# Gate and up projections by seven block products for eight, in one planned order with the first down blocks

## The chip, the cores and the metric

The kernel runs on one core of a Trainium2 chip. Its engines are TensorE (PE, with its weight loads as PEld), VectorE (DVE), ScalarE (ACT), GpSimd (POOL) and SyncE (SP), which issues the DMAs. The metric is the device time of one execution in microseconds (us), lower being better; the median of several runs is given with its spread.

## What is computed

One layer of a streaming encoder, on 1024 prompt frames and 32 sample frames (T = 1056 together), with a model width of 1024, 8 attention heads, 8 retention heads and a feed-forward width of 2816. All inputs and outputs are float32.

```python
h   = rmsnorm(x, g_norm);  z = h @ w_in            # q, k, v, retention q, k, v, gates
mix = sigmoid(gate_a) * diff_attention(...) + sigmoid(gate_r) * retention(...)
x   = x + mix @ w_o
h   = rmsnorm(x, g_ffn)
x   = x + (silu(h @ w_ff_gate) * (h @ w_ff_up)) @ w_ff_down
gate = sigmoid(rmsnorm(x, g_ple) @ w_ple_gate)
x   = x + gate * (p @ w_ple)
```

The change is in the lines from `x + mix @ w_o` to the product with `w_ff_down`.

## The kernel before, in words

**Precision.** TensorE gets float16 operands. Each float32 matrix is scaled by a power of two and split into a high and a low float16 part, and a product is made of three matmuls: high by high, high by low, low by high (`mm3`, L440 to L443). The scale of a block of weights comes from its largest magnitude: a reduction on DVE, then `partition_all_reduce` on POOL (L285), then a few one-column operations on DVE (`weight_scale`, L278). In the attention stage the scales of the input weights come from sums of squares (L393) that are spread over the partitions through TensorE (`spread_max`, L257).

**Attention stage.** Input projection, attention, retention and their gates are written as generators that say what they need next (an engine and an estimated time, a buffer, an event). The class `Flow` (L80) orders them: it always takes the step that can start first, and among equals the one with the lower priority number, and the instructions go to PE, DVE, ACT and POOL in that order under `manual_schedule` (L1384). At the end come the products for the last gate (`ple`, L1277), while the output weights `wo` (L1216, L1225) are loaded.

**Output projection** (from 1104.85 us on). Activations lie transposed, 128 features on the partitions and frames along the row. Three chunks c of 352 columns, and for each eight output blocks m of 128 features: 8 x 3 matmuls of 352 columns into a PSUM bank. DVE adds x (L1451), the sum goes to DRAM (`x1_d`, L1453), ACT squares it (L358), DVE sums the squares (L360). The norm of a chunk (`norm_steps`, L319) runs while TensorE works on the next: four column sums on TensorE (L328), DVE (L331), the power -0.5 on POOL (L333), a diagonal on DVE (L335), a broadcast on TensorE (L342); then the chunk is scaled and split into `xh1` (L349, L350, L352).

**Gate and up.** 22 blocks j of 128 features, loaded in 11 pairs (`load_gu`, L1398: DMA L1404, reduction L1406, splits L1410 and L1411). For each block and each of three chunks, a gate product and an up product of 8 x 3 matmuls of 352 columns (`gu_mm`, L1421), then `gu_out` (L1471): tanh on ACT (L1474), two products on DVE (L1475, L1476), a high part on ACT (L1478) and a low part on DVE (L1479), into `aT`, which holds all 22 blocks in SBUF.

**Down** (1679.18 to 1916.50 us). Eight output blocks m, three chunks, 22 x 3 matmuls of 352 columns each (L1520 to L1522); the weights of the next block (`load_dn`, L1481) are prepared meanwhile. The last gate follows.

Outside the attention stage the order is that of the framework, in the program's sequence, with the norm steps put between products by `step()` (L314). Three SBUF tiles hold split weights (`wtile`), two hold raw ones (`stage`), seven PSUM banks take products (`psb`, L1390) and one the sums (`pss`).

Of the kernel before, what the change touches and what calls it, by code (L numbers as in the profile page):

```python
# [33 lines left out]
NCH = 3  # L34
EPS = 1e-6
# [8 lines left out]
def _f(x):  # L44
    return float(x)
# [132 lines left out]
def kernel(  # L178
# [35 lines left out]
    mix_d = dram.tile([H, P, 2, T], F16, name="mix_d")  # L214

# [41 lines left out]
    def spread_max(amax, n, tag):  # L257


        yield ("wait", "id")  # L260
        yield ("get", "o")
        yield M(0.1)
        pt = ps_o.tile([P, 512], F32, tag="o", name="mt")
# [14 lines left out]
    def weight_scale(amax, n, gi, tag, pool=True, norm=False):  # L278
# [3 lines left out]
        if pool:  # L282
            yield G(0, 0.1)
            ar = sm(n, tag + "ar", 3)
            nc.gpsimd.partition_all_reduce(ar, amax, P, ABSMAX)  # L285
            yield from p2of(p2, ar, n, tag)
        else:
            ar = yield from spread_max(amax, n, tag)
            yield from p2of(p2, ar, n, tag, norm)
            yield ("put", "o")  # L290
# [4 lines left out]
        nc.vector.tensor_scalar(out=s, in0=s, scalar1=_f(2.0 ** -50) if norm else 16384.0, scalar2=None, op0=ALU.mult)  # L295
        d = sm(n, tag + "d", 6)
        if gi is None:
            nc.vector.tensor_scalar(out=d, in0=p2, scalar1=_f(2.0 ** -14), scalar2=None, op0=ALU.mult)
# [20 lines left out]
    def norm_steps(acc, dg, tag, split, late=0):  # L319

        pending.extend([lambda: None] * late)
        B = CH // 4
        box = []

        def first():
            ps = pss.tile([P, 512], F32, tag="ss", name="ss")
            for b in range(4):
                nc.tensor.matmul(out=ps[0:B, CH + b:CH + b + 1], lhsT=acc[:, b * B:(b + 1) * B], rhs=ones32[:, 0:1],  # L328
                                 start=True, stop=True)
            v = sm(4, tag + "v")  # L330
            nc.vector.tensor_scalar(out=v[0:B], in0=ps[0:B, CH:CH + 4], scalar1=_f(1.0 / D), scalar2=EPS, op0=ALU.mult, op1=ALU.add)  # L331
# [8 lines left out]
        def second():  # L340
            ps, d = box
            nc.tensor.matmul(out=ps[:, 0:CH], lhsT=ones32[0:B], rhs=d[0:B], start=True, stop=True)  # L342
            split(ps[:, 0:CH])
# [10 lines left out]
    def square_sum(pool, xf, k0, k1, acc):  # L354

        for k in range(k0, k1):
            sq = acc if k == 0 else pool.tile([P, CH], F32, tag="sq", name="sq")
# [97 lines left out]
    with ExitStack() as pa:  # L455
# [83 lines left out]
        def const_b():  # L539
# [10 lines left out]
            yield ("delay", 2.0)  # L550

# [760 lines left out]
        def stream():  # L1312
# [85 lines left out]
    def load_gu(jp):  # L1398
        w = wtile()[:, 0:KD * 1024].rearrange("p (j u a k c) -> p j u a k c", j=2, u=2, a=2, k=KD)
        hds = []  # L1400
        for jj in range(2):
            j = 2 * jp + jj
            st = stage()[:, 0:KD * 256].rearrange("p (k u c) -> p k u c", k=KD, u=2)
            nc.sync.dma_start(out=st, in_=wgu[j])  # L1404
            am = sm(2, "gam2", 3)
            nc.vector.tensor_reduce(out=am, in_=st.rearrange("p k g c -> p g k c"), axis=AX.XY, op=ALU.max,  # L1406
                                    apply_absolute_value=True)
            s, d = weight_scale_now(am, 2, 1, "gu")
            for u in range(2):
                nc.scalar.activation(w[:, jj, u, 0], st[:, :, u], AF.Copy, scale=s[:, u:u + 1])  # L1410
                nc.vector.scalar_tensor_tensor(out=w[:, jj, u, 1], in0=st[:, :, u], scalar=s[:, u:u + 1],  # L1411
                                               in1=w[:, jj, u, 0], op0=ALU.mult, op1=ALU.subtract)

            nc.vector.tensor_scalar(out=rf[:, j:j + 1], in0=d[:, 0:1], scalar1=_f(2.0 ** 55), scalar2=d[:, 1:2],
                                    op0=ALU.mult, op1=ALU.mult)
            hd = sm(1, "hdg", 6)
            nc.vector.tensor_scalar(out=hd, in0=d[:, 0:1], scalar1=0.5, scalar2=None, op0=ALU.mult)
            hds.append(hd)
        return w, hds

    def gu_mm(wt, jj, c):  # L1421
        cs = slice(c * CH, (c + 1) * CH)
        out = []
        for u in range(2):
            ps = bank()
            for k in range(KD):
                mm3(ps, wt[:, jj, u, 0, k], wt[:, jj, u, 1, k], xh1[:, k, 0, cs], xh1[:, k, 1, cs], k == 0, k == KD - 1)
            step()
            out.append(ps)
        return out  # L1430

    with ExitStack() as pb:
        wk = pb.enter_context(DT(name="wkB", bufs=2))
        xc = pb.enter_context(DT(name="xcB", bufs=2))
        wos = tail["wos"]

        mixs = xh1 = tail["mixs"]
        for c in range(NCH):
            c0 = c * CH
            xf = xc.tile([P, KD, CH], F32, tag="xf", name="xf")  # L1440
            nc.sync.dma_start(out=xf, in_=xT[:, :, c0:c0 + CH])
            acc = wk.tile([P, CH], F32, tag="acc", name="acc")
            for m in range(KD):
                ps = bank()
                wt, d = wos[m // 4]
                ms = slice(m % 4 * P, (m % 4 + 1) * P)
                for k in range(KD):
                    mm3(ps, wt[:, k, 0, ms], wt[:, k, 1, ms], mixs[:, k, 0, c0:c0 + CH], mixs[:, k, 1, c0:c0 + CH],
                        k == 0, k == KD - 1)
                step()  # L1450
                nc.vector.scalar_tensor_tensor(out=xf[:, m], in0=ps, scalar=d[m % 4 // 2], in1=xf[:, m],  # L1451
                                               op0=ALU.mult, op1=ALU.add)
                nc.sync.dma_start(out=x1_d[m, :, c0:c0 + CH], in_=xf[:, m])  # L1453
                square_sum(wk, lambda k: xf[:, k], m, m + 1, acc)

            def split(rs, c0=c0, xf=xf):
                for k in range(KD):
                    split_x(wk.tile([P, CH], F32, tag="sx", name="sx", bufs=4), xh1[:, k, 0, c0:c0 + CH], xh1[:, k, 1, c0:c0 + CH],
                            xf[:, k], k, rs, 1)

            norm_steps(acc, lambda: wk.tile([P, CH], F32, tag="dg", name="dg"), "nb", split, 1)
        nxt = load_gu(0)
        ahead = [gu_mm(nxt[0], 0, c) for c in range(2)]


    with ExitStack() as pc:
        apool = pc.enter_context(DT(name="apool", bufs=1))
        wk = pc.enter_context(DT(name="wkC", bufs=2))
        aT = apool.tile([P, NF, 2, T], F16, name="aT")

        def gu_out(j, c, hd, pg, pu):  # L1471
            cs = slice(c * CH, (c + 1) * CH)
            th = wk.tile([P, CH], F32, tag="sq", name="th")
            nc.scalar.activation(th, pg, AF.Tanh, scale=hd)  # L1474
            nc.vector.scalar_tensor_tensor(out=th, in0=th, scalar=1.0, in1=pg, op0=ALU.add, op1=ALU.mult)  # L1475
# [213 lines left out]
```

## Time and profile before

| | |
|---|---|
| runs, median | 2012.34 us of 3 (2011.31 to 2012.55) |
| the profiled execution | 2011.19 us, its span 2009.2 us |
| granted TensorE clock, mean | 0.994 |
| PE busy | 1953.9 us, 97% |
| DVE busy | 1328.2 us, 66% |
| ACT busy | 925.7 us, 46% |
| POOL busy | 553.8 us, 28% |
| DMA | 137.52 MB, 68 GB/s in the mean |
| matmul instructions recorded | 13577 |

Busy is the time in which an engine has at least one instruction under way. Matmuls overlap, and a row's duration of one matmul is longer than the distance to the next start; so paces are read from starts. A few per cent of matmul records are missing in a trace, so counts come from the code. A row of the timeline gives start, length, engine, line, operation, result and operands, count, and in brackets the idle time of the engine before it with what ended it.

### The profile page before, as it was taken

The page shows a single profiled execution, that of the slowest core. Times are in us where ns is not written, and L with a number is a line of the kernel's source. Part 1 is how long each engine was busy: PE and PEld are TensorE (multiplying, and loading weights), DVE is VectorE, ACT ScalarE, POOL GpSimd, SP SyncE. Part 2 cuts the span into 40 slices and gives each one's busy share as a digit, 9 for nine tenths or more (in the row PEclk, how much of TensorE's full clock was granted, in tenths as well). Part 3 has the DMA queues.
Part 4 walks back from the last instruction along what each step waited for, and adds up shares of the span by engine and source line. Part 5 has one row for each costly group of instructions (what it writes and reads, how often), then busy time and mean ns, then how long its engine had stood idle before and what let it go on. Part 6 is the DMA issues. An engine that isn't in the chain of part 4 may idle for free.

```text
span 2009.2 us, 35867 instructions
## 1 busy us (share of the span) xinstructions
PE 1953.9 (97%) x13577; PEld 1204.5 (60%) x13577; DVE 1328.2 (66%) x3465; ACT 925.7 (46%) x2406; POOL 553.8 (28%) x1059
## 2 busy tenths in 40 slices
PE   5899999999999999999999999999999999999999
PEld 2465565655655555555565566666666666666665
DVE  6887878787777877877987666454445543543364
ACT  6676666666666666666665233222223221111132
POOL 4654445454453545444441011000000000000010
PEclk9999999999999999999999999999999999999999
DMA  5121202112021111211216431211111103111131
GB/s 190 69 71 51 80 25 65 54 52 67 26 74 57 47 62 32 75 59 28 81 32 243 160 118 46 81 43 42 43 43 53 49 29 116 58 58 43 43 123 51
DMA packets 67148, 137.52 MB, mean 68 GB/s; under 512 B 24832, under 2 KB 49536, under 8 KB 59040
## 3 DMA queue, kind: packets, MB, share of 16 engines
q1 hardware_dynamic: 66976, 135.25, 20.3%
q8 instruction: 106, 1.74, 0.4%
q14 instruction: 66, 0.54, 0.1%
HBM read 108.74 MB, written 26.48 MB: 67 GB/s over the span
## 4 chain that ended last, share of the span: by engine, by line
PE 81%; DVE 9%; ACT 3%; POOL 3%; DMA 2%; issue 1%; SPq 0%; POOLq 0%; ACTq 0%; DVEq 0%
PE ps L441 10%; PE ps L442 10%; PE ps L443 10%; PE pj L688 8%; PE pj L690 8%; PE pj L689 8%; PE ps L1522 4%; PE ps L1521 4%; PE ps L1520 4%; PE sc L825 2%; PE sc L828 1%; PE t L872 1%; PE pj L699 1%; PE t L1020 1%; ACT p L843 1%
## 5 line engine op out<-in xcount | busy, mean ns | idle before, releaser
L441 PE MATMUL ps<-mixs,w 128*128 128x352 f16 x1248 | 391.5, 314 | 1.5 <-DVE pws L1298 1.5
L689 PE MATMUL pj<-w,xh 128*128 128x512 f16 x1024 | 389.6, 381 | 3.1 <-DVE w L434 3.1
L688 PE MATMUL pj<-w,xh 128*128 128x512 f16 x1024 | 390.8, 382 | 1.8 <-ACT w L432 1.8
L442 PE MATMUL ps<-mixs,w 128*128 128x352 f16 x1248 | 391.3, 314 | 0.0
L443 PE MATMUL ps<-mixs,w 128*128 128x352 f16 x1248 | 391.2, 313 | 0.0
L690 PE MATMUL pj<-w,xh 128*128 128x512 f16 x1024 | 389.6, 380 | 0.0
L441 PEld LDWEIGHTS <-w 128*128 128x128 f16 x1488 | 146.3, 98 | 79.5 <-DVE pws L1298 1.9
L442 PEld LDWEIGHTS <-w 128*128 128x128 f16 x1488 | 146.1, 98 | 77.3 <-issue 1.3
L443 PEld LDWEIGHTS <-w 128*128 128x128 f16 x1488 | 146.1, 98 | 77.3
L690 PEld LDWEIGHTS <-xh 128*128 128x128 f16 x1024 | 100.5, 98 | 125.8 <-issue 6.1
L1522 PE MATMUL ps<-aT,w 128*128 128x352 f16 x528 | 165.0, 313 | 0.0
L1521 PE MATMUL ps<-aT,w 128*128 128x352 f16 x528 | 165.0, 313 | 0.0
L1520 PE MATMUL ps<-aT,w 128*128 128x352 f16 x528 | 165.0, 313 | 0.0
L843 ACT ACTIVATE p<-sc,nb,scs 128x256 f32<-128x256 f32 (+7 forms) x128 | 106.1, 829 | 99.4 <-POOL nb L837 66.4
L688 PEld LDWEIGHTS <-xh 128*128 128x128 f16 x1024 | 101.2, 99 | 72.6 <-issue 1.0
L689 PEld LDWEIGHTS <-xh 128*128 128x128 f16 x1024 | 100.6, 98 | 71.6 <-issue 2.9
L1478 ACT ACTIVATE aT<-th 128x352 f16<-128x352 f32 x66 | 32.5, 494 | 201.2 <-DVE th L1476 195.4
L835 DVE TENSOR_REDUCE nm<-sc 128x2 f32<-128x256 f32 (+6 forms) x112 | 102.8, 918 | 23.5 <-PE sc L828 23.2
L285 POOL PARTITION_ALL_REDUCE guar<-gam x22 | 8.9, 406 | 364.5 <-DVE gam L1406 351.6
L1476 DVE SCALAR_TENSOR_TENSOR th<-th,ps 128x352 f32<-128x352 f32 x66 | 34.3, 519 | 101.8 <-PE ps L443 101.7
L1475 DVE SCALAR_TENSOR_TENSOR th<-th,ps 128x352 f32<-128x352 f32 x66 | 34.2, 518 | 89.7 <-ACT th L1474 89.6
L1474 ACT ACTIVATE th<-ps,hdg 128x352 f32<-128x352 f32 x66 | 36.2, 550 | 114.1 <-PE ps L443 113.8
(400 smaller groups left out, 4209.5 us busy)
## 6 DMA issues: line engine op xcount, KB each, us to landing
st<-in_win_dram SPq DMA_DIRECT2D x30, 1024.0 KB, 4.9
st<-in_wgu_dram SPq DMA_DIRECT2D x22, 1024.0 KB, 5.1
st<-in_wdn_dram SPq DMA_DIRECT2D x16, 704.0 KB, 4.4
out_dram<-kv SPq DMA_DIRECT2D x64, 128.0 KB, 1.7
mixs<-mix_d SPq DMA_DIRECT2D x8, 528.0 KB, 6.8
pw_d<-pws SPq DMA_DIRECT2D x12, 352.0 KB, 3.6
xf<-in_xT_dram SPq DMA_DIRECT2D x3, 1408.0 KB, 7.2
x_d<-xf SPq DMA_DIRECT2D x24, 176.0 KB, 2.2
```

What stands on the lines that cost most here:

```text
L441: nc.tensor.matmul(out=ps, lhsT=wh, rhs=ah, start=first, stop=False)
L442: nc.tensor.matmul(out=ps, lhsT=wh, rhs=al, start=False, stop=False)
L443: nc.tensor.matmul(out=ps, lhsT=wl, rhs=ah, start=False, stop=last)
L688: nc.tensor.matmul(out=ps, lhsT=xhi, rhs=w[:, k, 0], start=(k == 0), stop=False)
L689: nc.tensor.matmul(out=ps, lhsT=xhi, rhs=w[:, k, 1], start=False, stop=False)
L690: nc.tensor.matmul(out=ps, lhsT=xh[:, k, 1, t0:t0 + P], rhs=w[:, k, 0], start=False, stop=(k == KD - 1))
L825: nc.tensor.matmul(out=o, lhsT=q4[:, m, 0:R], rhs=kts[:, m], start=True, stop=False)
L835: nc.vector.tensor_reduce(out=nm[0:R, mc], in_=pv, axis=AX.X, op=ALU.max, negate=True)
L843: nc.scalar.activation(pt[0:R, 0:NK], ps[0:R, p0:p0 + NK], AF.Exp, bias=nb[0:R, m:m + 1], scale=sc_ap[0:R], accum_out=Z[0:R, m:m + 1])
L1520: nc.tensor.matmul(out=ps, lhsT=wt[:, 0, j], rhs=aT[:, j, 0, cs], start=(j == 0), stop=False)
L1521: nc.tensor.matmul(out=ps, lhsT=wt[:, 1, j], rhs=aT[:, j, 0, cs], start=False, stop=False)
L1522: nc.tensor.matmul(out=ps, lhsT=wt[:, 2, j], rhs=aT[:, j, 1, cs], start=False, stop=(j == NF - 1))
```

## The change

The work from the output projection to the second down block is one `Flow` of its own.

- **Seven products.** A block j of weights is seen as two by two quarters (gate or up, by lower or upper half of the 1024 inputs), a pair of column chunks as two by two quarters of the activations. Seven products of sums of quarters (the Strassen-Winograd scheme) replace eight. A product is 4 x 3 matmuls of 264 columns: T is cut into four chunks of `CW` = 264, which make two pairs p.
- **Weights** (`load_gu`): POOL makes four sums of quarters (512 columns each, `comb_w`), seven operands are split (`split`: ACT and DVE, 512 columns each). The scale comes from two Square sums on ACT, two matmuls with a matrix of ones (`total=True` in `weight_scale`) and the one-column operations on DVE.
- **Activations** (`residual`, `sums`, `parts16`): after the norm, sums of quarters are made on DVE or POOL, whichever is free first in the plan, and split by ACT and DVE or POOL, into `xh1` and new tiles `tT`.
- **Products** (`gu_pair`) and their sums (`gu_sums`): per pair two copies on ACT and seven additions on DVE, then `gu_out` for each half, now from SBUF.
- **Order**: (0,0), (1,0), (0,1), (1,1), then (j,0), (j,1); block j + 2 is asked for when block j begins.
- **Down**: the first two output blocks are prepared in the same order (`load_dn`) and start on rows 8 to 21 of the 22; rows 0 to 7 have gone to DRAM (`a_d`) and come back after the last pair, and then complete the six sums that wait in PSUM. From the third output block on, everything is as before.
- **Before the stage**: at the last head the weights of `ple` are loaded ahead of the first `wo` pair, instead of behind. Two constants of the second norm are scaled by 0.25 and 16.

```diff
+CW = 264
+NW = 4
+NS = 14
...
+    a_d = dram.tile([NF - NS, P, 2, T], F16, name="a_d")
...
-    def weight_scale(amax, n, gi, tag, pool=True, norm=False):
+    def weight_scale(amax, n, gi, tag, pool=True, norm=False, total=False, at_bank=None):
...
+        if total:
+            yield ("get", "ss")
+            yield M(0.3)
+            ps = pss.tile([P, 512], F32, tag="ss", name="ss")
+            for i in range(2):
+                nc.tensor.matmul(out=ps[:, 0:1], lhsT=ones32, rhs=amax[:, i:i + 1], start=i == 0, stop=i == 1)
+            yield ("delay", 0.3)
+            yield from p2of(p2, ps[:, 0:1], n, tag, norm)
+            yield ("put", "ss")
...
-                        flow.add(load_wo_0(), 0)
-                        flow.add(load_ple(), 1)
+                        flow.add(load_ple(), 0)
+                        flow.add(load_wo_0(), 1)
...
+            def residual(c):
+                p, odd = divmod(c, 2)
...
+                yield G(4, 0.2)
+                r = sm(4, "nbr")
+                nc.gpsimd.tensor_tensor(out=r[0:B], in0=v[0:B], in1=neghalf[0:B], op=ALU.pow)
+                yield V(CW)
+                dg = wkb.tile([P, CW], F32, tag="dg", name="dg")
...
+                yield M(0.5)
+                nc.tensor.matmul(out=ps[:, 0:CW], lhsT=ones32[0:B], rhs=dg[0:B], start=True, stop=True)
...
+            def split(j, w, s, i, src):
+                yield S(HK * P, 0.18)
+                nc.scalar.activation(w[:, i, 0], src, AF.Copy, scale=s)
+                yield ("delay", 0.4)
+                yield V(HK * P, 1.0, 0.06)
+                nc.vector.scalar_tensor_tensor(out=w[:, i, 1], in0=src, scalar=s, in1=w[:, i, 0], op0=ALU.mult, op1=ALU.subtract)
+                yield ("set", ("gw", j, i))
+
+            def comb_w(out, in0, in1, op):
+                yield G(HK * P, 0.1)
+                nc.gpsimd.tensor_tensor(out=out, in0=in0, in1=in1, op=op)
+                yield ("delay", 0.6)
+
+            def load_gu(j):
+                yield ("get", "st")
+                st = stage()[:, 0:KD * 256].rearrange("p (k u c) -> p k u c", k=KD, u=2)
+                yield DM(1.0)
+                nc.sync.dma_start(out=st, in_=wgu[j])
+                yield ("delay", 2.0)
+                yield ("get", "w")
+                yield ("delay", 0.6)
...
+                for i in range(2):
+                    yield S(1024, 0.3)
+                    nc.scalar.activation(w[:, S3 + i].bitcast(BF16), st[:, i * HK:(i + 1) * HK].rearrange("p k u c -> p u k c"),
+                                         AF.Square, accum_out=am2[:, i:i + 1])
+                yield ("delay", 1.0)
+                s, d = yield from weight_scale(am2, 1, 1, "gu", norm=True, total=True)
...
+                flow.add(split(j, w, s, A1, q1), 1)
+                flow.add(split(j, w, s, A2, q2), 1)
+                flow.add(split(j, w, s, A4, q4), 1)
+                yield from comb_w(tmp, q1, q3, ALU.subtract)
+                yield from comb_w(q3, q3, q4, ALU.add)
+                flow.add(split(j, w, s, S1, q3), 1)
...
+            def gu_sums(j, p):
...
+                def comb(out, in0, ps, op=ALU.add):
+                    yield V(CW, 1.0, 0.06)
+                    nc.vector.tensor_tensor(out=out, in0=in0, in1=ps, op=op)
...
+            def gu_pair(j, p):
+                ca, cb = (slice((2 * p + i) * CW, (2 * p + i + 1) * CW) for i in range(2))
+                ops = dict(x1=(xh1, 0, ca), t1=(xh1, 0, cb), x3=(xh1, HK, ca), x4=(xh1, HK, cb))
+                yield ("get", "pr")
+                flow.add(gu_sums(j, p))
+                for n, (i, b) in enumerate(((A1, "x1"), (S1, "t1"), (A2, "x3"), (S2, "t2"), (A4, "t4"), (S4, "x4"), (S3, "t3"))):
+                    yield ("wait", ("gw", j, i))
+                    for k in range(HK):
+                        yield ("wait", ("o", p, b, k))
+                    yield ("get", "ps")
+                    yield M(1.35)
...
+                        mm3(ps, w[:, i, 0, k], w[:, i, 1, k], hi, lo, k == 0, k == HK - 1)
...
+                for m in range(2):
+                    yield ("wait", ("dn", m))
+                    for js in (range(NF - NS, 15), range(15, NF)):
+                        for c in range(NCH):
...
+            flow = Flow(dict(ps=7, ss=1, w=3, st=2, pr=2, th=2, acc=2, sq=2))
...
+        for j in range(NF - NS):
+            nc.sync.dma_start(out=back[j], in_=a_d[j])
...
+        nxt = load_dn_now(2)
+        for m in range(2):
+            for c in range(NCH):
+                down_mm(halves[m, c], dns[m][0], range(NF - NS), c, first=False)
+                down_out(halves[m, c], dns[m][1], m, c)
```

More of the change, by code (lines that the diff above doesn't have):

```diff
@@ L317, in step, with norm_steps @@
             pending.pop(0)()
-    def norm_steps(acc, dg, tag, split, late=0):
+    def norm_steps(acc, dg, tag, split, late=0, W=CH):
         pending.extend([lambda: None] * late)
-        B = CH // 4
+        B = W // 4
         box = []
@@ L341, in second @@
             ps, d = box
-            nc.tensor.matmul(out=ps[:, 0:CH], lhsT=ones32[0:B], rhs=d[0:B], start=True, stop=True)
-            split(ps[:, 0:CH])
+            nc.tensor.matmul(out=ps[:, 0:W], lhsT=ones32[0:B], rhs=d[0:B], start=True, stop=True)
+            split(ps[:, 0:W])
         pending.extend((first, second))
@@ L550, in const_b @@
             yield ("delay", 2.0)
+            yield V(24)
+            nc.vector.tensor_scalar(out=gS[:, 1], in0=gS[:, 1], scalar1=0.25, scalar2=None, op0=ALU.mult)
+            yield V(1)
+            nc.vector.tensor_scalar(out=gd[:, 1:2], in0=gd[:, 1:2], scalar1=16.0, scalar2=None, op0=ALU.mult)
             gam = sm(2, "gam")
@@ L1396 @@
     rf = const.tile([P, NF], F32, name="rf")
[L1398 to L1451, printed above, removed]
-                                               op0=ALU.mult, op1=ALU.add)
[L1453 to L1463, printed above, removed]
@@ L1554 @@
             for c in range(NCH):
-                down(m, c)
+                ps = bank()
+                down_mm(ps, dn[0], range(NF), c)
+                down_out(ps, dn[1], m, c)
                 if m + 1 == KD and c == 1:
```

354 lines of the change are left out of this document (304 added, 50 removed).

## The prediction

> **What bounds the kernel now.** I read first the page's span, busy shares and chain, then the stretches by stage, and last the waits of TensorE inside the stages that change.
>
> ```profile
> span 2009.2 us, 35867 instructions
> ...
> PE 81%; DVE 9%; ACT 3%; POOL 3%; DMA 2%; issue 1%; SPq 0%; POOLq 0%; ACTq 0%; DVEq 0%
> ```
>
> ```profile
> 100.00:1000.00 900.00, 892.62 (x6483) 520.29 (x6482) 721.99 (x2204) 591.41 (x1744) 427.49 (x854) 1.00 0.18 56
> 1104.85:1679.18 574.33, 566.56 (x3776) 370.74 (x3777) 290.55 (x541) 141.84 (x228) 24.29 (x40) 0.99 0.18 62
> 1679.18:1916.50 237.32, 237.32 (x1595) 155.85 (x1593) 106.33 (x173) 35.12 (x45) 6.82 (x13) 1.00 0.19 67
> ...
> 1230.00:1670.00 440.00, 440.00 (x2952) 288.61 (x2951) 206.01 (x377) 104.00 (x163) 8.56 (x21) 1.00 0.13 44
> ```
>
> Columns: stretch, its length, busy PE, PEld, DVE, ACT, POOL, clock, DMA share, GB/s. TensorE carries 81% of the chain. The change lies in 1104.85 to 1679.18: output projection, then gate and up. Between 1230 and 1670 TensorE never stops while DVE works 206 of 440 us, so only fewer TensorE cycles shorten this stage, and half of DVE is free to pay for them. The first row is the attention stage: the same kind of planned order as the change brings, DVE 80% busy, POOL 47%, and TensorE still 99.2%.
>
> **The change part by part.**
>
> *Price of a matmul.* Starts, not durations, give the pace, since matmuls overlap:
>
> ```profile
> 92.87 0.38 PE L688 MATMUL pj<-w,xh 128*128 128x512 f16 x1
> ...
> 94.60 0.38 PE L690 MATMUL pj<-w,xh 128*128 128x512 f16 x1
> ...
> 310.38 0.27 PE L828 MATMUL sc<-kT,q 128*128 128x256 f16 x1
> 310.49 0.27 PE L825 MATMUL sc<-kT,q 128*128 128x256 f16 x1
> ```
>
> ```profile
> L1522 PE MATMUL ps<-aT,w x528: 311/313/313, 1679.2 to 1916.2; 128*128 128x352 f16 x176
> ```
>
> 512 columns: 1.73 us over 8 steps, 0.216 us. 352 columns: L1520 to L1522 are 1584 matmuls whose starts span 237.0 us, 0.1497 us. The slope is 0.0666/160 = 0.000416 us a column, so 264 columns cost 0.1497 - 88 x 0.000416 = 0.1131 us. The 256-column row, 0.11 us with a weight load of its own, lies next to it and leaves no room for a large fixed price.
>
> Gate and up: before 22 x 3 x 2 x 24 = 3168 matmuls of 352, 474.2 us. After 22 x 2 pairs x 7 products x 12 = 3696 of 264, 418.0 us: **-56.2**. Output projection: 576 x 0.1497 = 86.2 becomes 768 x 0.1131 = 86.9: **+0.7**. The down matmuls stay 1584 of 352 columns; their order changes, their sum doesn't.
>
> The Trainium skill, "TensorE: Matmul & The Clock Gate", section Back-to-back issue gap, speaks against this: streams with a weight load each settle at about 81 ns for 128 columns and 131 ns for 512. My estimate on its line is 110 ns at 352 and 99 ns at 264, hence 349 us before and 365 after, +16 instead of -56. The trace doesn't agree: its 0.150 and 0.216 us stand where that line has 0.110 and 0.131.
>
> *TensorE work added.* The scales go through two f32 matmuls with a ones matrix per block; nearest are the four of L328:
>
> ```profile
> 1140.66 0.71 PE L328 MATMUL ss<-cst_sb,acc 128*88 128x1 f32 x8
> 1141.23 0.31 PE L441 MATMUL ps<-mixs,w 128*128 128x352 f16 x1
> ```
>
> 0.57 us for four, so 0.28 for two and 22 x 0.28 = **+6.3** (ends: 0.03 us a matmul, the gap from 310.35 to 310.38 for 64 columns, gives 1.3; twice the price gives 12.6). A fourth norm, four columns sums (0.57) and a broadcast of about 0.6: **+1.2**. Two down scales through TensorE instead of POOL, by the same row about 0.3 each: **+0.6**.
>
> *Stalls removed.*
>
> ```profile
> 1104.85 0.32 PE L441 MATMUL ps<-mixs,w 128*128 128x352 f16 x1 [1.50 <-DVE pws L1298]
> ...
> 1149.66 1.54 PE L342 MATMUL ss<-dg,cst_sb 88*128 88x352 f32 x2 [4.68 <-DVE dg L335]
> ...
> 1214.72 0.93 PE L342 MATMUL ss<-dg,cst_sb 88*128 88x352 f32 x2 [3.09 <-DVE dg L335]
> ...
> 1148.00 1.05 POOL L333 TENSOR_TENSOR nbr<-nbv,neghalf 88x4 f32<-88x4 f32 x1 [7.65 <-issue]
> ```
>
> ```profile
> 1150.00:1155.00 5.00, 5.00 (x20) 2.54 (x20) 3.86 (x9) 2.52 (x6) 1.60 (x2) 0.61 0.10 36
> 1155.00:1160.00 5.00, 5.00 (x35) 3.31 (x34) 3.46 (x8) 2.35 (x5) 2.34 (x3) 1.00 0.30 91
> 1215.00:1220.00 5.00, 5.00 (x22) 2.63 (x22) 5.00 (x8) 1.94 (x4) 0.00 (x0) 0.66 0.44 184
> ```
>
> Two norms make TensorE wait 4.68 and 3.09 us, and behind each wait the clock is 0.61 and 0.66 for a stretch: 20 and 22 matmuls where 35 fit, some 13 x 0.15 = 2.0 us each. Together **-11.8** for the norms as they are now. The first wait has POOL late with nothing released to it ("issue"), just after its all-reduces for the scales; the change has no such all-reduce left in this stage. The 1.50 us at the start stay, since the banks are still handed over from the last ple product.
>
> *Stalls added.* The norms stay chains TensorE - DVE - POOL - DVE - TensorE. The plan gives POOL's power 0.36 us; the row above shows 1.05. So each of four norms may find TensorE 0.7 us early: **+2.8** (0 to 8). Queued behind the waiting broadcast are the next products; seven banks are of no help there, as the wait is in TensorE's own order; POOL's power may itself stand behind a sum of a block's weights.
>
> The first block's scale matmul is the one whose data can be late:
>
> ```profile
> 1109.64 0.42 SPq L1404 DMA_DIRECT2D st<-in_wgu_dram  x1
> ...
> 1116.98 2.29 DVE L1406 TENSOR_REDUCE gam<-st 128x2 f32<-128x2048 f32 x1 [0.59 <-DMA st<-in_wgu_dram]
> ```
>
> That transfer took 7.3 us while the DMA engines were full. It now stands in SP's order behind two chunks of x but ahead of the first write of x1, so it is issued at about 1105 to 1110 and lands at 1112 to 1117; two squares add some 2.5 us. By the plan's costs the matmul sits about four output blocks (4 x 24 x 0.1131 = 10.9 us) into the stage, at 1115.7. TensorE waits 0 to 4 us, plus the slow clock: **+3**. At pair (0,1) DVE has to be through the last norm, its operand sums, two blocks' splits and two pairs' sums; TensorE covers this with two pairs, 2 x 84 x 0.1131 = 19.0 us. I take **+2** (0 to 8). For the planned order as a whole I take the attention stage's loss, 0.8% of 505 us: **+4**.
>
> *The other engines, per block of two pairs (19.0 + 0.3 = 19.3 us of TensorE).*
>
> ```profile
> 1151.24 1.56 DVE L349 SCALAR_TENSOR_TENSOR sx<-xf,gS,ss 128x352 f32<-128x352 f32 x3 [1.14 <-PE ss L342]
> ...
> 1157.26 0.51 DVE L360 TENSOR_TENSOR acc<-acc,sq 128x352 f32<-128x352 f32 x1
> 1157.70 0.57 DVE L1451 SCALAR_TENSOR_TENSOR xf<-ps,o1d,xf 128x352 f32<-128x352 f32 x1
> ...
> 1210.51 2.48 DVE L1411 SCALAR_TENSOR_TENSOR w<-st,gus,w 128x1024 f16<-128x1024 f32 x2 [0.49 <-ACT w L1410]
> ...
> 1208.52 0.16 DVE L223 TENSOR_SCALAR guc<-guar 128x2 f32<-128x2 f32 x1
> ...
> 1209.44 0.51 DVE L1476 SCALAR_TENSOR_TENSOR th<-th,ps 128x352 f32<-128x352 f32 x1
> ```
>
> From PSUM an operation of 352 holds DVE 0.495 us ((1.56 - 0.57)/2), from SBUF 0.44 (1157.26 to 1157.70); at 0.96 elements a ns (1024 in 1.20 us from the pair of L1411 less 352 in 0.495) 264 cost 0.40 and 0.35. A split of 512 costs 1.20 - 0.53 = 0.67. Per block: 12 sums from PSUM 4.8, 14 operations from SBUF 4.9, 7 splits 4.7, seven small ones 0.92: 15.3 us, 79% of 19.3, the attention stage's share. ACT has two squares, 7 splits, and 12 operations of 264:
>
> ```profile
> L393 ACT ACTIVATE w<-st 128x1024 bf16<-128x1024 f32 x54 | 57.2, 1059 | 0.0
> ...
> 1217.39 1.47 ACT L350 CAST mixs<-sx 128x352 f16<-128x352 f32 x3 [5.16 <-DVE sx L349]
> ```
>
> At most 2 x 1.3 + 7 x 0.7 + 12 x 0.5 = 13.5 us, no bound. POOL has four sums of 512:
>
> ```profile
> L638 POOL TENSOR_TENSOR w<-w 128x1024 f32<-128x1024 f32 x7 | 16.7, 2383 | 11.8 <-ACT xsq L633 11.8
> ...
> 1152.96 0.99 POOL L352 TENSOR_TENSOR mixs<-sx,mixs 128x352 f16<-128x352 f32 x1 [3.92 <-ACT mixs L350]
> ...
> 1153.65 0.68 DVE L352 TENSOR_TENSOR mixs<-sx,mixs 128x352 f16<-128x352 f32 x1
> ```
>
> About 1.2 us each, half of the 1024-wide row, 4.8 a block. But the DVE row shows a price: 0.68 us for what takes 0.51, and it ends 0.38 after POOL's own end at 1153.95, as if it had started only then. I take 0.7 us a block (7% on the 9.6 us with two SBUF inputs): DVE 16.0, covered. If all 4.8 were lost, DVE has 20.1.
>
> *Hidden edits.* Loads run one to two blocks (19 to 38 us) ahead. SP issues 32 writes of x1 for 24, eight rows out and eight back; nothing on TensorE waits for a write. Past the last pair, 12 half groups of 21 matmuls (37.7 us) cover eight rows read back and two of x1, ten times 528 KB, 5.4 MB: at the 320 GB/s that the DMA engines reached around 1080 to 1105, 17 us; below 144 GB/s they would show. The tail of attention gets its ple and output weights in another order: 0 (-3 to +3).
>
> ```profile
> 1079.00:1104.85 25.85, 24.35 (x152) 14.82 (x149) 19.15 (x59) 17.44 (x39) 0.77 (x2) 0.94 0.92 320
> ```
>
> **Sum**, against the profiled execution's 2011.19 us (span 2009.2 and 2.0 around it): -56.2 + 0.7 + 6.3 + 1.2 + 0.6 - 11.8 + 2.8 + 3 + 2 + 4 = -47.4, so 1963.8. The median of the runs, 2012.34, is 1.15 higher: 1965.
>
> **The rivals.** (a) *DVE and POOL shut each other out and DVE becomes the bound.* For: the DVE row at 1153.65. Against: the attention stage, with POOL at 47%. With the whole 4.8 us, DVE takes 20.1 us a block against 19.3: 22 x 0.8 = 18 more, 1983. By the Trainium skill, "SBUF — State Buffer", section SBUF: two separate sides, this is so: a VectorE operation with two SBUF inputs and a GpSimd one that reads SBUF hold one port for the whole instruction. The trace agrees in that one row's 0.68 us.
>
> (b) *Slower: TensorE waits for each block's scale.* The matmul on the sums of squares stands in TensorE's order with products behind it, where POOL's all-reduce kept no one. If the squares come late by d in every block, 22 d is lost; from d = 47/22 = 2.1 us on nothing is gained, at 2.5 us the time is 2020. Against it:
>
> ```profile
> PE t L1182 <- POOL mx L1178: 2.3, 5, 0.5
> ...
> st<-in_wgu_dram SPq DMA_DIRECT2D x22, 1024.0 KB, 5.1
> ```
>
> The longest list entry of TensorE's waits between 100 and 1080 us, where scales go through TensorE likewise, is 2.3 us; and a block's weights, 5.1 us to land, are asked for a block ahead.
>
> (c) *A matmul has a large fixed price*, and 17% more of them eat the gain: from 474.2/3696 = 0.128 us on for 264 columns, the stage gains nothing, and the time is 1965 + 56 = 2021. The 256-column row, 0.11, is against it. By the estimate on the Trainium skill's line above it would be 2037.
>
> **How the numbers follow.** Forecast 0.72, 1950 to 1976 by the ends above (cheap scales -5, no waits -12; waits doubled +12). Rival (a) 0.20, 1977 to 1993. Rival (b) 0.06, two thirds of it beyond 2012. Rival (c) 0.02, half of it beyond. The range 1950 to 1990 leaves out 0.1 or so above and little below. About 0.2% (4 us) is what a measurement here can tell from no change: faster 0.94, same 0.01, slower 0.05.
>
> **What would show it.** 264-column matmuls with starts 0.113 us apart; some 530 us from the first output matmul to the first down matmul; DVE at 80 to 85% there, POOL at 25 to 30%; TensorE's waits in that stretch under 20 us, at norms and scales. Wrong if: starts above 0.12; DVE above 95% with TensorE waiting for it block by block; a wait before each scale.

## The result, and the profile after

The changed kernel takes 1966.56 us (median of four runs, 1965.34 to 1967.29) against 2011.97 for the kernel before (2011.31 to 2012.55): a ratio of 0.9774, with a 95% interval of 0.9757 to 0.9791. The profiled execution took 1965.95 us.

The page of the changed kernel begins with its span; the second line is the chain that ended last, by engine:

```profile
span 1964.1 us, 38704 instructions
...
PE 84%; DVE 7%; ACT 4%; POOL 3%; issue 1%; DMA 1%; SPq 0%; POOLq 0%; DVEq 0%; ACTq 0%
```

TensorE carries 84% of the chain where it carried 81%. The next view is the table of stretches of the changed kernel (length, then busy time of PE, PEld, DVE, ACT and POOL, each with its count, then clock, DMA share, GB/s). The first row is output projection with gate and up, the second the down products, the third a steady part of gate and up; the five of 5 us show the clock: 47 matmuls fit at clock 1.00, and 27, 33 and 36 ran in stretches at or behind a wait; in the one from 1225 TensorE waits most of the time.

```profile
1104.46:1632.60 528.14, 520.82 (x4595) 451.08 (x4595) 467.65 (x1020) 285.24 (x599) 179.17 (x147) 0.99 0.22 73
1632.60:1870.90 238.30, 238.00 (x1597) 155.90 (x1596) 122.25 (x199) 41.64 (x53) 8.82 (x15) 1.00 0.26 92
1260.00:1600.00 340.00, 339.98 (x3037) 296.61 (x3035) 323.33 (x715) 200.51 (x409) 105.47 (x72) 1.00 0.20 66
1105.00:1110.00 5.00, 5.00 (x27) 3.41 (x26) 0.49 (x2) 0.00 (x0) 0.00 (x0) 0.54 0.96 341
...
1110.00:1115.00 5.00, 5.00 (x47) 4.36 (x45) 1.95 (x3) 2.92 (x6) 2.44 (x2) 1.00 0.71 212
...
1180.00:1185.00 5.00, 4.91 (x33) 3.78 (x34) 0.94 (x3) 0.42 (x1) 1.01 (x1) 0.66 0.12 42
...
1225.00:1230.00 5.00, 1.85 (x12) 1.46 (x12) 5.00 (x11) 2.63 (x8) 4.19 (x6) 0.90 0.00 0
1230.00:1235.00 5.00, 5.00 (x36) 3.88 (x34) 4.94 (x11) 0.85 (x2) 2.22 (x2) 0.76 0.00 0
```

The whole gain lies in the first row: 574.33 us before, 528.14 now, 46.2 less. The start of the stage moved by 0.4 us (1104.85 to 1104.46), the down products are 1.0 us longer (237.32 to 238.30), and what follows them took 92.7 us before and 93.2 now. In the third row TensorE works 339.98 of 340 us while DVE works 323.33, 95%.

What TensorE waited for between 1000 us and the end (us in total, times, longest; the attention stage's last wait, 0.5 us, and two of 0.3 us are left out), and rows of its timeline:

```profile
PE ps L459 <- ACT pws L1319: 5.1, 1, 5.1
PE ps L460 <- DVE mixs L1463: 3.9, 2, 2.4
PE ss L1521 <- DVE acc L1514: 3.3, 1, 3.3
```

```profile
1104.46 0.38 PE L459 MATMUL ps<-mixs,w 128*128 128x264 f16 x1 [5.08 <-ACT pws L1319]
...
1109.63 0.28 PE L459 MATMUL ps<-mixs,w 128*128 128x264 f16 x1
...
1109.97 0.28 PE L459 MATMUL ps<-mixs,w 128*128 128x264 f16 x1
...
1278.85 0.68 PE L295 MATMUL ss<-gam,cst_sb 128*128 128x1 f32 x4
...
1585.85 0.50 PE L295 MATMUL ss<-gam,cst_sb 128*128 128x1 f32 x4
```

Four waits are left: the hand-over of the banks from the ple product, the third chunk's sum of squares (L1521, at 1180), and twice the operands of pair (0,1), at 1226 and 1229. Neither the scale matmuls (L295) nor the norms' broadcasts (L1535) stand in the list. At full clock three steps take 0.34 us, 0.113 a matmul of 264 columns. From the last two rows, 16 blocks take 307.0 us, 19.19 each: 168 matmuls make 19.00 of it, the scale 0.19.

### The profile page after: what moved, and what is told of

It reads as the page before. It is cut to its first block, busy times and chain, and to the rows that moved or that the text cites. A ratio compares the mean times of both kernels' runs of the same rounds, so it can differ in the third digit from the quotient of the medians.

```text
span 1964.1 us, 38704 instructions
## 1 busy us (share of the span) xinstructions
PE 1908.1 (97%) x14401; PEld 1284.3 (65%) x14401; DVE 1524.3 (78%) x3982; ACT 1074.5 (55%) x2774; POOL 715.8 (36%) x1168
## 4 chain that ended last, share of the span: by engine, by line
PE 84%; DVE 7%; ACT 4%; POOL 3%; issue 1%; DMA 1%; SPq 0%; POOLq 0%; DVEq 0%; ACTq 0%
PE ps L459 10%; PE ps L460 10%; PE ps L461 10%; PE pj L711 9%; PE pj L712 8%; PE pj L713 8%; PE ps L1443 4%; PE ps L1442 4%; PE ps L1441 4%; PE sc L848 2%; PE sc L851 2%; PE t L895 2%; PE t L1043 1%; PE pj L722 1%; PE po L914 1%
## 5 line engine op out<-in xcount | busy, mean ns | idle before, releaser
L459 PE MATMUL ps<-mixs,w 128*128 128x264 f16 x960 | 267.4, 279 | 5.1 <-ACT pws L1319 5.1
L460 PE MATMUL ps<-mixs,w 128*128 128x264 f16 x960 | 267.4, 279 | 3.9 <-DVE mixs L1463 3.9
L461 PE MATMUL ps<-mixs,w 128*128 128x264 f16 x960 | 267.4, 279 | 0.0
L460 PEld LDWEIGHTS <-w 128*128 128x128 f16 x1728 | 169.9, 98 | 40.1 <-issue 5.7
L461 PEld LDWEIGHTS <-w 128*128 128x128 f16 x1728 | 169.9, 98 | 39.5 <-issue 4.3
L459 PEld LDWEIGHTS <-w 128*128 128x128 f16 x1728 | 172.0, 100 | 34.8 <-issue 0.2
L1558 POOL TENSOR_TENSOR st<-st 128x512 f32<-128x512 f32 x66 | 97.0, 1470 | 250.9 <-DVE w L1553 168.4
L1553 DVE SCALAR_TENSOR_TENSOR w<-st,gus,w 128x512 f16<-128x512 f32 x132 | 147.5, 1119 | 0.0
L459 PE MATMUL ps<-tT,w 128*128 128x264 f16 x528 | 145.9, 276 | 0.0
L460 PE MATMUL ps<-tT,w 128*128 128x264 f16 x528 | 145.8, 276 | 0.0
L461 PE MATMUL ps<-tT,w 128*128 128x264 f16 x528 | 145.7, 276 | 0.0
L1442 PE MATMUL ps<-a,w 128*128 128x352 f16 x336 | 105.0, 313 | 0.3 <-DVE w L1638 0.3
L1443 PE MATMUL ps<-a,w 128*128 128x352 f16 x336 | 105.0, 313 | 0.0
L1441 PE MATMUL ps<-a,w 128*128 128x352 f16 x336 | 105.0, 313 | 0.0
```

Source lines behind the costliest of these rows:

```text
L459: nc.tensor.matmul(out=ps, lhsT=wh, rhs=ah, start=first, stop=False)
L460: nc.tensor.matmul(out=ps, lhsT=wh, rhs=al, start=False, stop=False)
L461: nc.tensor.matmul(out=ps, lhsT=wl, rhs=ah, start=False, stop=last)
L1441: nc.tensor.matmul(out=ps, lhsT=wt[:, 0, j], rhs=a[:, 0, cs], start=(first and j == js[0]), stop=False)
L1442: nc.tensor.matmul(out=ps, lhsT=wt[:, 1, j], rhs=a[:, 0, cs], start=False, stop=False)
L1443: nc.tensor.matmul(out=ps, lhsT=wt[:, 2, j], rhs=a[:, 1, cs], start=False, stop=(last and j == js[-1]))
```

## The experiments

All were timed beside the kernel before on the same chip; ratios are to it.

**e1, eight products.** The change with plain products: no operand sums, no weight sums, 4992 matmuls of 264 columns in place of 4464.

```diff
-                for n, (i, b) in enumerate(((A1, "x1"), (S1, "t1"), (A2, "x3"), (S2, "t2"), (A4, "t4"), (S4, "x4"), (S3, "t3"))):
...
+                for h, cs in enumerate((ca, cb)):
+                    for u, qs in enumerate(((A1, A2), (S1, A4))):
...
+                                mm3(ps, w[:, qs[k // HK], 0, k % HK], w[:, qs[k // HK], 1, k % HK], xh1[:, k, 0, cs], xh1[:, k, 1, cs],
+                                    k == 0, k == KD - 1)
```

> The seven products and their operand sums are replaced by the plain eight (four sums of two quarters in PSUM per pair of chunks), everything else of the change stays. Theory (the gain is TensorE columns): 22 x 2 x 8 x 12 = 4224 matmuls of 264 for 3696, 528 x 0.1131 = 60 us more, less some 5 for the waits at pair (0,1), which has no sums to wait for: about 2021, so no faster than the kernel before; DVE near half busy. Rival (the gain is mostly the planned order and the removed waits, or DVE and not TensorE sets the pace of the seven): at most 40 us more than 1966, under 2006.

It took 2013.07 us, ratio 1.0007 (0.9998 to 1.0016): the time of the kernel before. Its table of stretches:

```profile
1105.00:1680.00 575.00, 574.92 (x5120) 500.34 (x5120) 244.38 (x636) 213.49 (x429) 22.21 (x28) 1.00 0.20 67
1260.00:1600.00 340.00, 340.00 (x3037) 296.59 (x3035) 129.27 (x351) 124.26 (x248) 0.00 (x0) 1.00 0.17 59
```

TensorE does not pause in 575 us, with DVE at 129 of 340 us and POOL idle. So everything in the change but the trade of eight products for seven cancels out: the norms' old waits go (-11.8), and smaller tiles (4992 x 0.1131 - 3744 x 0.1497 = +4.1), the scales (+4.1), the fourth norm and the down scales (+1.8, the forecast's figure) and slow clock at the start take it back. The products left out are the gain: 528 x 0.1131 = 59.7 us, of which the changed kernel keeps 2013.07 - 1966.56 = 46.5. Of the 13.2 lost, 7.2 us are its waits at L1521 and L460, which this kernel doesn't have, and 2.8 the slow clock behind them; some 3 us are in no row that was read. The theory's 2021 took off only 5 us for all of that.

**e2, the weight sums on DVE.**

```diff
             def comb_w(out, in0, in1, op):
-                yield G(HK * P, 0.1)
-                nc.gpsimd.tensor_tensor(out=out, in0=in0, in1=in1, op=op)
+                yield V(HK * P)
+                nc.vector.tensor_tensor(out=out, in0=in0, in1=in1, op=op)
```

> The four sums of weight quarters per block go from POOL to DVE. Theory (POOL's sums shut DVE's two-input operations out): DVE's splits, 1137 ns in the mean between 1260 and 1600 us, fall back to about 745, and DVE pays 4 x 0.6 = 2.4 us a block for the sums instead of about 3 us of waiting: DVE still 90 to 95% busy, the time within 4 us of 1966. Rival (the splits are long for another reason): they stay above 1000 ns, DVE has 18.4 + 2.4 = 20.8 us of work a block against 19.3 of TensorE, and the time grows by 22 x 1.5 = 33 us, to about 1999.

1967.18 us, ratio 0.978 (0.9766 to 0.9793): no different from the changed kernel. DVE's groups between 1260 and 1600 (busy us, mean ns of one), of the changed kernel and then of this one:

```profile
L1553 DVE SCALAR_TENSOR_TENSOR w<-st,gus,w 128x512 f16<-128x512 f32 x110 | 125.0, 1137 | 0.0
L1679 DVE TENSOR_TENSOR snu<-snu,ps 128x264 f32<-128x264 f32 x105 | 44.1, 420 | 6.1 <-PE ps L461 3.9
...
L1553 DVE SCALAR_TENSOR_TENSOR w<-w,gus 128x512 f16<-128x512 f32 x18 | 28.5, 1586 | 0.0
```

```profile
L1553 DVE SCALAR_TENSOR_TENSOR w<-st,gus,w 128x512 f16<-128x512 f32 x109 | 81.3, 746 | 0.0
L1679 DVE TENSOR_TENSOR snu<-snu,ps 128x264 f32<-128x264 f32 x105 | 44.9, 427 | 11.1 <-PE ps L461 9.7
L1558 DVE TENSOR_TENSOR st<-st 128x512 f32<-128x512 f32 x55 | 37.7, 685 | 0.0
...
L1558 DVE TENSOR_TENSOR w<-st 128x512 f32<-128x512 f32 x18 | 13.6, 757 | 0.0
L1553 DVE SCALAR_TENSOR_TENSOR w<-w,gus 128x512 f16<-128x512 f32 x18 | 13.4, 746 | 0.0
```

A split, with both inputs in SBUF, takes 746 ns in the mean without POOL's sums and 1137 or 1586 with them; an addition with an input in PSUM (L1679) takes 420 and 427. The price of POOL's help is 110 x 0.391 + 18 x 0.840 = 58 us of DVE in 340, more than the 37.7 + 13.6 = 51 us that the sums take on DVE itself. A timeline of the changed kernel shows the blocking, and the row below it the spread of the 18 splits with the longer mean (least, median and greatest ns):

```profile
1399.71 1.32 POOL L1558 TENSOR_TENSOR st<-st 128x512 f32<-128x512 f32 x1 [0.69 <-DVE w L1553]
1399.83 1.75 DVE L1553 SCALAR_TENSOR_TENSOR w<-st,gus,w 128x512 f16<-128x512 f32 x1
...
1404.37 0.74 DVE L1553 SCALAR_TENSOR_TENSOR w<-st,gus,w 128x512 f16<-128x512 f32 x1
```

```profile
L1553 DVE SCALAR_TENSOR_TENSOR w<-w,gus x18: 737/1754/1759, 1265.2 to 1582.1; 128x512 f16<-128x512 f32 x18
```

POOL's sum runs from 1399.71 to 1401.03. The split that starts 0.12 us into it ends at 1401.58, 0.55 us past POOL's end, of the 0.74 us that the undisturbed one needs in all. By the Trainium skill, "SBUF — State Buffer", section SBUF: two separate sides, whichever of the two starts first keeps the shared port for its whole instruction; these rows agree, but for the 0.2 us by which the split ends sooner than if it had begun only then.

The means mix two kinds. Of the 128 splits of the changed kernel between 1260 and 1600, 69 start while a sum of POOL runs, and each of them ends 0.55 us after that sum's end; the other 59 take 0.74 to 0.75 us. POOL pays as well. At L1694 DVE adds two tiles of SBUF in 0.42 us, with or without a sum of POOL beside it; the 33 sums that it meets take 1.32 to 1.97 us instead of 1.26, and end 1.12 to 1.14 us after it, even where their record starts 0.3 to 0.4 us before its own; so the order of the records' starts doesn't always say which of the two goes first. The operation with an input in PSUM keeps its 0.41 to 0.43 us in the 27 cases in which it starts during a sum of POOL.

**e3, the scales by POOL's all-reduce again.**

```diff
-            for i in range(2):
-                nc.tensor.matmul(out=ps[:, 0:1], lhsT=ones32, rhs=amax[:, i:i + 1], start=i == 0, stop=i == 1)
...
+            nc.vector.tensor_tensor(out=am1, in0=amax[:, 0:1], in1=amax[:, 1:2], op=ALU.add)
+            yield G(0, 0.3)
+            nc.gpsimd.partition_all_reduce(ar, am1, P, bass_isa.ReduceOp.add)
```

> The scale of a block goes through an all-reduce on POOL again instead of two matmuls with ones. Theory (POOL pays some 6 us when it turns from an all-reduce to another operation, as in the kernel before, and here it has sums in every block): 22 x 0.28 = 6 us of TensorE are saved, but POOL shows gaps of about 6 us with no releaser in every block, one or two of them, and its work comes to 12 to 18 of 19.3 us; loads run a block or two ahead, so the time lies between 1960 and 1985. Rival (no such price): 1960, and no gaps.

2002.99 us, ratio 0.9961 (0.995 to 0.9973): 36 us slower than the changed kernel, and worse than either theory had it. POOL's rows, its configuring instructions between 1260 and 1600, and TensorE's waits:

```profile
1270.30 0.41 POOL L295 PARTITION_ALL_REDUCE gam<-gam  x1 [8.19 <-DVE gam L293]
1278.62 1.26 POOL L1556 TENSOR_TENSOR w<-st 128x512 f32<-128x512 f32 x1 [7.92 <-issue]
1279.96 2.62 POOL L1556 TENSOR_TENSOR st<-st 128x512 f32<-128x512 f32 x2
1288.56 0.40 POOL L295 PARTITION_ALL_REDUCE gam<-gam  x1 [5.98 <-issue]
1296.33 1.25 POOL L1556 TENSOR_TENSOR st<-st 128x512 f32<-128x512 f32 x1 [7.37 <-issue]
```

```profile
L1556 POOLq MODIFY_POOL_CONFIG  x34: 82/83/83, 1270.7 to 1587.3; - x34
```

```profile
PE ss L1519 <- DVE acc L1512: 11.6, 3, 4.7
PE ps L458 <- POOL tT L1461: 9.1, 1, 9.1
PE ps L457 <- ACT snq L1683: 7.6, 1, 7.6
PE ps L457 <- DVE snq L1677: 5.3, 12, 1.1
```

At each turn from all-reduce to sum or back POOL stands for 6 to 8 us, in three of these four rows with nothing released to it ("issue"); two turns a block and five instructions fill its 19.2 us. So it is in all 34 turns between 1260 and 1600 (5.98 to 8.19 us): most of the gaps are put down to another engine, but their lengths keep to that band. At the head of each stand two instructions MODIFY_POOL_CONFIG, 94 in this kernel's trace and 6 in the changed kernel's. Such a pair, and 7.65 us, stood in front of the old norm's power at 1148.00 too. The Trainium skill, "GPSIMD Engine Reference", section 2.1 Instruction dispatch, puts about 6 us on the first call of a freshly loaded kernel, without a visible instruction; the gaps have that size, but no run here shows that it is loading.

Little of the 36 us is lost in the steady blocks: of TensorE's waits, 24.8 us lie between the stage's first matmul and 1260, where POOL has operand sums as well (7.2 in the changed kernel; the clock there is 0.90 in the mean), 10.6 between 1260 and 1400, and 2.6 between 1400 and 1600.

**e4, four more sums on POOL in each block.**

```diff
-                yield from comb_w(tmp, q1, q3, ALU.subtract)
+                for _ in range(5):
+                    yield from comb_w(tmp, q1, q3, ALU.subtract)
```

> The first sum of weight quarters on POOL is made five times instead of once, with the same result: eight sums a block for four. Theory (each POOL sum shuts out DVE, 3 us a block now, and DVE is at 95%): some 6 us a block, DVE 15.3 + 6 = 21.3 against 19.3 of TensorE, so DVE becomes the bound: up to 22 x 2 = 44 us more, 1985 to 2010, with TensorE waiting for DVE block by block. Rival (TensorE still sets the pace, the waits are hidden): within 5 us of 1966.

2073.25 us, ratio 1.031 (1.0296 to 1.0324): 107 us more, far beyond either. Its waits of TensorE, one of POOL's between 1260 and 1600, and two of its stretches:

```profile
PE ps L461 <- DVE w L1553: 49.9, 14, 4.8
PE ps L459 <- ACT w L1550: 17.5, 9, 2.7
```

```profile
POOL w L1558 <- DMA st<-in_wgu_dram: 97.5, 8, 14.2
```

```profile
1260.00:1600.00 340.00, 291.18 (x2418) 243.72 (x2419) 312.11 (x572) 160.98 (x330) 160.87 (x114) 0.92 0.16 55
...
1405.00:1410.00 5.00, 2.98 (x14) 2.09 (x15) 4.97 (x11) 1.50 (x4) 0.41 (x1) 0.50 0.00 0
```

Now TensorE waits for splits in every second block, some 6 us in two waits, which is much like what rival (a) described; around such a pair the granted clock falls to 0.50 to 0.61 for a stretch, and behind waits of less than half a microsecond it stays at 1.00. From 1300 us on the pairs come 47.7 us apart, so a block takes 23.8 us, 4.6 more than before, while DVE's work grows to 21.9 us (312.11 of 340 busy), 2.7 over the old 19.2. DVE is thus not full. The edit also lengthens the chain from a block's load to its last split, and POOL waits 97.5 us for weights to land, so loads come late as well. No run parts the two causes, nor shows at how much more work the waits begin.

**The waits at the head of the stage.** e5 to e12 try to take back the 12 us that stand there.

e5 makes the order of pairs (0,0), (1,0), (2,0), (0,1) and so on, to give pair (0,1) one pair more of cover:

```diff
-                for j, p in [(0, 0), (1, 0), (0, 1), (1, 1)] + [(j, p) for j in range(2, NF) for p in range(2)]:
+                for j, p in [(j, p) for p in range(2) for j in range(3)] + [(j, p) for j in range(3, NF) for p in range(2)]:
```

> The pairs begin (0,0), (1,0), (2,0), (0,1), (1,1), (2,1), and a block is asked for earlier to match. Theory (at pair (0,1) TensorE waits for operand sums of the last chunk that DVE and POOL have not finished): a third pair covers 9.5 us more, the waits of 3.9 us at L1463 and the slow clock after them go, 1966.5 becomes 1961. Rival (DVE is short of time over the whole stage, so the wait only moves): the wait shows up later and the time stays within 2 us.

1978.02 us, ratio 0.983 (0.9817 to 0.9844): 12 slower. The wait for operands is gone, and the third block's splits, of ACT and of DVE, are late in its place; DVE is busy in all of the 20 us from 1220 to 1240:

```profile
PE ps L459 <- ACT w L1550: 6.6, 2, 4.1
PE ps L461 <- DVE w L1553: 6.1, 2, 3.1
```

e6 gives the ple evacuations the highest priority, e7 the operand sums of the first two chunks a lower one, e8 is e5, e6 and e7 together.

```diff
+                        yield ("prio", -1)
                         g = yield either(S(CH), V(CH))
+                        yield ("prio", 6)
```

```diff
-                        flow.add(sums(c, k - HK))
+                        flow.add(sums(c, k - HK), 1 if p == 0 else 0)
```

> The copies that empty the banks of the ple products get the first place in the plan, ahead of the splits of the last output weights. Theory (these copies stand on ACT behind the splits, and the first output product waits 5.1 us for the last of them): the wait falls under 1.5 us and the 2 us of slow clock after it go: 1966.5 becomes 1960. Rival (the last row of mix, or the second pair of output weights, comes late as well): the wait stays above 3 us or moves to the fifth product, and less than 2 us are gained.

> The operand sums of the first two chunks get a later place in the plan than the norm and the sums of squares of the third. Theory (the third chunk's norm is late, TensorE waits 3.3 us at L1521, because DVE works off 36 operand sums first): the wait goes and some 1.6 us of slow clock with it: 1961.5. Rival (the wait comes from POOL's power or from the plan's figure for it): unchanged, 1966.5.

> The three edits of the runs beside it together. If the three waits are separate, the gains add: 5.5 + 6.5 + 5 = 17, but not more than the 11.5 us by which the stage stands above its matmuls, and 5 before it: 1950 to 1954. If DVE is short over the whole stage: above 1958.

They took 1966.37 (0.9771, 0.9758 to 0.9785), 1966.0 (0.9773, 0.9759 to 0.9786) and 1977.94 us (0.9827, 0.9814 to 0.9841), the last being the time of e5. In e6 the start wait is 4.9 us, in e7 that at L1521 is still 3.3: a priority in the planner only breaks ties between steps that could start at the same time, so neither moved its wait, and neither tests a cause.

e9 loads the first output weights ahead of the ple weights, as before the change; e10 holds the operand sums of the first two chunks (16 sums and 20 splits) until the third chunk's last output block is planned; e11 gives all 24 ple evacuations to DVE; e12 is e10 and e11 together.

```diff
-                        flow.add(load_ple(), 0)
-                        flow.add(load_wo_0(), 1)
+                        flow.add(load_wo_0(), 0)
+                        flow.add(load_ple(), 1)
```

```diff
                 p = c // 2
+                if not p:
+                    yield ("wait", ("wo", 2, KD - 1))
```

```diff
-                        g = yield either(S(CH), V(CH))
+                        g = yield V(CH)
```

> The changed kernel with the first output weights loaded ahead of the ple product's weights again, as before the change. Theory (the swap is needed, because the first gate and up block takes over the tile that is free first, and it now holds the ple weights): the first block's weights come some 10 us later, TensorE waits 5 to 15 us ahead of pair (0,0), total 1971 to 1982; the start wait falls from 5.1 to the 1.5 us of the kernel before. Rival (the swap is what makes the start wait 5.1 us, and the first block has time enough): 1961 to 1964.

> The 36 operand sums of the first two chunks are started only when the third chunk's last output block is in the list, so that they cannot stand ahead of the third chunk's sum of squares. Theory (the 3.3 us wait of TensorE for that sum is DVE's: the operand sums fill it, slowed by GpSimd): the wait goes, with the slow clock behind it, total 1961 to 1964, unless pair (0,0) then waits for its operands. Rival (it moves: the sums end some 10 us later, and pair (0,0) or (1,0) waits for operands by 3 us or more): 1966 to 1972.

> All 24 evacuations of the ple product go to DVE, none to ACT. Theory (the start wait of 5.1 us is that of an evacuation which stands behind the output weights' splits in ACT's order): the wait falls to 2 us or less, the slow clock behind it is shorter, total 1961 to 1964. Rival (it is the five buffers that the ple product's transfers hold, or the psum banks, whatever engine evacuates): the wait stays at 4 to 5.5 us, now for DVE, total 1965 to 1968.

> The last two edits together. Theory (two waits that are independent): 1957 to 1962, the sum of what the two gain alone. Rival (one wait takes up what the other gives back): no better than the better of the two by itself, 1962 to 1967.

e9: 1966.26 us, ratio 0.978 (0.9762 to 0.9798), the time of the changed kernel; neither theory. Its start:

```profile
1103.08 0.29 PE L459 MATMUL ps<-mixs,w 128*128 128x264 f16 x1 [1.50 <-DVE pws L1321]
```

It starts 1.4 us sooner and at full clock (47 matmuls between 1105 and 1110), but TensorE had stood 2.2 us longer between 1060 and 1080 (17.3 of 20 us busy for 19.5), and later waits 1.6 us for scales and 1.1 for a down block's weights. So the swap of loads is what made the start wait longer, but only the place of the idle time differs; the first gate and up block comes in time in either order, but for 1.0 us at its scale.

e10: 1970.79 us, ratio 0.9803 (0.9787 to 0.982), 4 slower. The third chunk's sum no longer waits; the fourth's does, and longer. Its row, and the adds that lead to it as a group of DVE between 1190 and 1206:

```profile
1206.31 1.06 PE L1523 MATMUL ss<-cst_sb,acc 128*66 128x1 f32 x8 [4.79 <-DVE acc L1516]
```

```profile
L1516 DVE TENSOR_TENSOR acc<-acc,sq 128x264 f32<-128x264 f32 x5 | 4.8, 964 | 1.0 <-ACT sq L1513 1.0
```

Those adds take 964 ns each beside POOL's sums, 454 in the changed kernel over the same time. So the cause was the theory's, the operand sums ahead of the sum of squares (with them held, the third chunk's wait goes), and the outcome much like the rival's: the work has to be done ahead of pair (0,0), and the chunk beside it waits.

e11: 1968.24 us, ratio 0.979 (0.977 to 0.9809); the wait stays at 4.6 us, now for DVE, and the stage starts at 1106.47, 2 us later. Taking the evacuations out of ACT's order does not remove the wait; but DVE is then 21.28 of 24 us busy from 1080 to 1104, so its order may have taken the place of ACT's. The other candidate is the buffers that the ple product's transfers hold. In the changed kernel the evacuating engines sat idle for them in this tail:

```profile
  DMA pw_d<-pws: 3.4, 5
```

They take 5.5 us to land (median) where they took 3.6 before, and 3.2 in e9, whose start wait is 1.50. No run changed that alone, so this cause is argued and not shown.

e12: 1972.22 us, ratio 0.981 (0.9793 to 0.9826): the losses of e10 and e11 added. No version was found that is faster than the changed kernel.

## Why the prediction was right, and where its terms were not

The total came out 1.6 us above the forecast, and the stage at 528.1 where the sum gives 574.33 - 47.4 = 526.9. Point by point:

- **The price of a matmul** (0.1131 us at 264 columns from two pace rows): measured 0.113, and e1, with the eight products back, gives up the whole gain. Rival (c) is out; the 99 ns that the estimate on the Trainium skill's "TensorE: Matmul & The Clock Gate", section Back-to-back issue gap, gave for this width is not what this stream runs at.
- **The scales through TensorE** (+6.3): 0.19 us a block, 4.1. What the prediction did not price is what they spare: with them on POOL in this kernel, e3 loses 36 us. It had the sign of it in its own row, the 7.65 us of "issue" behind the all-reduces, and used it only for the old norm's wait.
- **The norms' waits** (-11.8, then +2.8 for the new ones): the old ones went (their slow clock, reckoned as 13 matmuls each, was 15 and 13, so 2.2 and 1.9 us). The new ones came to 3.3 us and some 1.6 of slow clock, not for POOL's power, as forecast, but ahead of it, for the adds on DVE (the wait's row names them, and in e10 it goes when the operand sums are held).
- **The first block's scale** (+3): nothing waits there. **Pair (0,1)** (+2): 3.9 us, and 1.2 of slow clock. DVE worked 9.94 of the 10 us from 1225 to 1235, and e5's order only put other waits in its place.
- **The planned order** (+4 by the attention stage's 0.8%): 0.02 us in 340; where the operands are there, it loses nothing.
- **The start wait** ("stay" at 1.50): 5.08. The start itself moved by only 0.4 us, since TensorE came to it 4.0 us earlier; what it cost is the clock behind it, 20 matmuls fewer in 5 us, 2.3 us.
- **The lock of DVE and POOL** ("I take 0.7 us a block"): this is the step of the working that failed. With 17.7 blocks in 340 us, DVE takes 323.33/17.7 = 18.3 us a block, not 16.0; without sums e2 gives (316.29 - 51.3)/17.7 = 15.0 where 15.3 was reckoned, so the lock is 3.3, two thirds of the way to the bound of 4.8. It cost no time because 18.3 still lies under 19.2. The one row that the prediction had, 0.68 us for 0.51, was an operation of 352 elements beside one of 0.99 us on POOL; splits of 512 beside sums of 1.3 us wait longer. DVE's share came to 95% in the steady part and 89% over the stage, not 80 to 85%, POOL's to 31% and 34%, above 25 to 30%.

So the waits and slow clock that were forecast, 2.8 + 3 + 2 + 4 = 11.8 us, came to 7.2 of waits and 2.3 + 1.6 + 1.2 of clock, 12.3: the sum was right and its items mostly were not, which is luck. Rival (a) had the mechanism right and stopped 0.9 us a block short of deciding. Its 18 us counted DVE's excess alone, and neither the slow clock behind the waits nor loads that then come late; in e4, where both are seen, a block lost 4.6 us with DVE 2.7 over TensorE. Rival (b) has no row in the changed kernel; in e4, e5 and e9 its wait appears with 1.1 to 3.8 us in all.

## What to carry to other kernels

In the steady part of this stage the trade of TensorE columns for sums on other engines was worth its columns, because every other engine stayed below TensorE's time per block. Their time has to be reckoned with DVE and POOL slowing each other: here POOL's help cost DVE 58 us to spare it 51. Look at what an engine pays to change between kinds of instruction (here POOL, sums and all-reduces) before it is given both in one loop. At the head of this stage a changed order (e5, e10) only moved the waits, and around one of them DVE had no time left.

## What the runs showed of the hardware

- POOL stands 6 to 8 us at each change between an all-reduce and a tensor operation (e3: 5.98 to 8.19 in 34 changes), with two instructions MODIFY_POOL_CONFIG at the head of the gap.
- A DVE split with its inputs in SBUF that starts during a sum of POOL ends 0.55 us after that sum (69 of 69), and takes 0.74 us otherwise; where DVE is ahead, POOL's sum waits (1.32 to 1.97 us for 1.26). A DVE operation with an input in PSUM stays at 0.42.
- In the changed kernel the waits of 5.08 and 3.3 us, and the two of 2.4 and 1.5 us taken together, are each followed by 5 us at a granted clock of 0.54, 0.66 and 0.76, and so cost 2.3, 1.6 and 1.2 us more than their length. Behind e9's wait of 1.50 us at the start the clock is 1.00.
